# One decoder block on one core: the attention output is multiplied by its norm before the output projection, and the memory values are formed 512 columns wide

## The chip, the cores and the metric

The kernel runs on one core of a Trainium2 chip. The metric is device time in microseconds (us) of one execution. The runs shown before the change took 800.42, 800.91 and 801.06 us, so the median is 800.91 us. All engine times below come from one profiled execution of the same kernel.

## What is computed

The block works on 512 tokens of 1024 features, in float32, in this order:

```python
u  = rmsnorm(h, g_mix)
qa, ka, va, qb, kb, vb = split(u @ w_in)            # 16 heads of 64
ya = dilated_attention(qa, ka, va, bias)            # heads 0..7
yb = moba_attention(qb, kb, vb, bias)               # heads 8..15
y  = concat(rmsnorm(ya, g_out_dil), rmsnorm(yb, g_out_moba))
h  = h + y @ w_out
h  = h + cross_attention(rmsnorm(h, g_cross), rmsnorm(mem, g_mem))   # 256 memory tokens, 4 heads
h  = h + w_down(silu(conv3(rmsnorm(h) @ w_gate)) * (rmsnorm(h) @ w_up))
out = rmsnorm(h, g_final)
```

Two norms stand between self-attention and `w_out`: one over the 512 features of heads 0 to 7, one over those of heads 8 to 15. A norm's factor is one number per token and half, so it can be multiplied into `y` before the product, or into the two half products after it.

## The kernel before

Everything is kept with features on the partitions and tokens on the free axis. A float32 product is made of three float32r matmuls: each operand is split into a rounded high part and the rest, and high x high, low x high and high x low are summed in one PSUM bank (`fgroup`, L263 to L268). Such a triple for one slice of 128 input features is called a group here.

**Weights.** `Weights` (L54 to L137) streams chunks of 128 x 1024 numbers through three buffers: a DMA from the queue of SyncE, then ScalarE writes the high part in two halves (L88), then VectorE or GpSimd writes the low part in two halves (L97). `tick(k)` issues these four pieces beside the groups of the chunk in use and stays two chunks ahead.

**Order.** The order of every engine's instructions is the order in which the program issues them. `Later` (L140) holds chains of small operations and issues each stage some steps behind: every group on TensorE ends with `L.step()`, and a stage is issued once its step number is reached. `drain` issues all that is left at once.

**PSUM.** There are eight banks: `acc` 2, `s` 3, `t` 2, `o` 1 (L190). A bank that is asked for again is handed over only when the reads of its former content have ended.

**Self-attention** runs in 18 slots. In slot s the scores of head s (S), the transposes of head s-1 (T) and the value product of head s-2 (O) are issued in the order given by `ORDER`, and between them projections that don't depend on attention are filled in: `fill(x)` issues groups until the count that `PACE` gives for slot x is reached. There are 208 such groups: Q, K and V projections (the first 144), memory keys `km_unit` (32), memory values `vm_unit` (32). `need` issues what is left after the last slot; before the change nothing is left. After a pair of heads, `o_evac` adds up `y`, squares it into a running sum and splits it into `Yh` and `Yl`, without the norm (L762 to L770).

**Memory values** (L574 to L609) are made in four column groups of 256 and two token tiles, one bank each, one after the other: a matmul has 256 columns.

**Output projection** (L819 to L842). Each of eight tiles takes two banks, one for each half of the features. The first is multiplied by the first norm on VectorE (f0) and added to `h` on GpSimd (L832); the second is multiplied by the second norm on VectorE (f1) and added to `h` on VectorE (L840). `resid` then makes the operand of the next product (ScalarE L251, VectorE L261) and the running sum of squares (ScalarE L276, GpSimd L281). The norm factors come from `norm_stages` (L283): a copy and a rest (L290, L294), two matmuls with ones (L301, L302), an inverse square root and a square on ScalarE (L306, L307), and three VectorE operations (L311 to L313). Cross-attention's query projection (`cq_unit`, L848) follows at once; its first tile needs `Xh[7]`, which comes from the last tile of the output projection.

**Later stages.** `w_o` (L984 to L1012) already runs its first three tiles over part of the features, holds them in three banks, and then finishes them.

## Time and profile before

| | |
|---|---|
| median of 3 runs | 800.91 us |
| span of the profiled execution | 799.3 us |
| what lies around the span (median minus span) | 1.6 us |
| groups of memory values left behind the last slot of attention | 0 |
| output projection, first matmul to first matmul of the next product | 260.75 to 305.69 us |

The profile lists no other time for the profiled execution than its span; the three runs stand 1.1 to 1.8 us above it. A matmul's row gives a modelled duration that overlaps the next matmul, so what one costs in a stream is read from the distance between the starts of neighbours, and a wait shows as a larger distance. "Idle before" in square brackets says how long the engine stood still and whom it waited for.

### The profile page before, as it was taken

The page shows a single profiled execution, that of the slowest core. Times are in us where ns is not written, and L with a number is a line of the kernel's source. Part 1 is how long each engine was busy: PE and PEld are TensorE (multiplying, and loading weights), DVE is VectorE, ACT ScalarE, POOL GpSimd, SP SyncE. Part 2 cuts the span into 40 slices and gives each one's busy share as a digit, 9 for nine tenths or more (in the row PEclk, how much of TensorE's full clock was granted, in tenths as well). Part 3 has the DMA queues.
Part 4 walks back from the last instruction along what each step waited for, and adds up shares of the span by engine and source line. Part 5 has one row for each costly group of instructions (what it writes and reads, how often), then busy time and mean ns, then how long its engine had stood idle before and what let it go on. Part 6 is the DMA issues. An engine that isn't in the chain of part 4 may idle for free.

```text
span 799.3 us, 10566 instructions
## 1 busy us (share of the span) xinstructions
PE 776.4 (97%) x3916; PEld 657.2 (82%) x3916; DVE 493.0 (62%) x894; ACT 389.8 (49%) x763; POOL 165.2 (21%) x163
## 2 busy tenths in 40 slices
PE   9999999999999998999999999999999999999995
PEld 7878989878898786888888888888888888888884
DVE  4656677678886987666476756666656664332324
ACT  5866666677767533544255533343334343322322
POOL 1056565663645343000021000000000000000001
PEclk9999999999999998999999999999999999999998
DMA  9544243343434222121033332222232233333303
GB/s 346 192 136 138 91 126 93 120 114 122 146 133 155 83 81 104 55 78 53 26 106 106 107 105 101 84 106 95 90 106 105 80 99 99 99 93 98 100 21 105
DMA packets 27107, 85.85 MB, mean 107 GB/s; under 512 B 3072, under 2 KB 5248, under 8 KB 26672
## 3 DMA queue, kind: packets, MB, share of 16 engines
q1 hardware_dynamic: 25696, 83.90, 31.7%
q10 hardware_dynamic: 1232, 1.12, 0.4%
q8 instruction: 30, 0.49, 0.3%
q14 instruction: 21, 0.17, 0.1%
q0 software_dynamic: 128, 0.17, 0.1%
HBM read 78.84 MB, written 2.14 MB: 101 GB/s over the span
## 4 chain that ended last, share of the span: by engine, by line
PE 77%; DVE 12%; ACT 6%; issue 2%; POOL 2%; DVEq 0%; POOLq 0%; ACTq 0%
PE acc L266 15%; PE acc L267 15%; PE acc L268 15%; PE s L266 5%; PE s L267 5%; PE s L268 5%; DVE lo L97 2%; ACT P L688 2%; DVE P L695 2%; PE o L739 1%; DVE tmp L257 1%; DVE P L683 1%; POOL h L832 1%; PE t L710 1%; ACT hi L88 1%
## 5 line engine op out<-in xcount | busy, mean ns | idle before, releaser
L88 ACT ACTIVATE hi<-stage 128x512 fp32r<-128x512 f32 (+1 forms) x264 | 151.7, 616 | 171.6 <-PE acc L267 130.7
L97 DVE TENSOR_TENSOR lo<-stage,hi 128x512 fp32r<-128x512 f32 (+1 forms) x211 | 156.8, 773 | 57.6 <-ACT hi L88 57.5
L266 PE MATMUL acc<-X,hi 128*128 128x512 f32 (+1 forms) x432 | 167.3, 387 | 3.6 <-ACT X L251 3.4
L268 PE MATMUL acc<-X,lo 128*128 128x512 f32 (+1 forms) x432 | 162.9, 377 | 0.0
L267 PE MATMUL acc<-X,hi 128*128 128x512 f32 (+1 forms) x368 | 137.6, 374 | 1.4 <-DVE X L261 1.2
L266 PEld LDWEIGHTS acc<-X,hi 128*128 128x128 f32 x432 | 82.3, 191 | 16.8 <-ACT X L251 3.8
L268 PEld LDWEIGHTS acc<-X,lo 128*128 128x128 f32 x432 | 82.1, 190 | 15.0
L267 PEld LDWEIGHTS acc<-X,hi 128*128 128x128 f32 x368 | 69.8, 190 | 12.6 <-DVE X L261 2.5
L97 POOL TENSOR_TENSOR lo<-stage,hi 128x512 fp32r<-128x512 f32 x53 | 71.6, 1368 | 27.3 <-ACT hi L88 25.7
L266 PE MATMUL acc<-G,hi 128*128 128x512 f32 (+1 forms) x198 | 72.9, 368 | 0.0
L268 PE MATMUL acc<-G,lo 128*128 128x512 f32 (+1 forms) x198 | 72.3, 365 | 0.0
L267 PE MATMUL acc<-G,hi 128*128 128x512 f32 (+1 forms) x198 | 72.3, 365 | 0.0
L266 PE MATMUL s<-X,hi 128*128 128x512 f32 x176 | 68.5, 389 | 0.0
L267 PE MATMUL s<-X,hi 128*128 128x512 f32 x176 | 68.5, 389 | 0.0
L268 PE MATMUL s<-X,lo 128*128 128x512 f32 x176 | 68.5, 389 | 0.0
L688 ACT ACTIVATE P<-P,st 128x512 f32<-128x512 f32 (+1 forms) x64 | 35.6, 557 | 39.9 <-DVE st L683 39.7
L1042 DVE SCALAR_TENSOR_TENSOR c<-a,vec,c 128x512 f32<-128x512 f32 x44 | 33.1, 752 | 24.6 <-ACT c L1037 23.8
L1032 POOL MEMSET a<- 128x2 f32 x22 | 2.1, 100 | 210.3 <-DVE c L1042 210.3
L281 POOL TENSOR_TENSOR ss<-ss,tmp 128x512 f32<-128x512 f32 x14 | 18.2, 1298 | 123.9 <-ACT tmp L276 123.9
L266 PEld LDWEIGHTS acc<-G,hi 128*128 128x128 f32 x198 | 37.3, 188 | 6.2
L267 PEld LDWEIGHTS acc<-G,hi 128*128 128x128 f32 x198 | 37.3, 188 | 6.1
L268 PEld LDWEIGHTS acc<-G,lo 128*128 128x128 f32 x198 | 37.3, 188 | 5.9
(242 smaller groups left out, 1516.4 us busy)
## 6 DMA issues: line engine op xcount, KB each, us to landing
stage<-in_w_gu_dram SPq DMA_DIRECT2D x44, 512.0 KB, 3.3
stage<-in_w_in_dram SPq DMA_DIRECT2D x23, 512.0 KB, 3.4
stage<-in_w_dn_dram SPq DMA_DIRECT2D x16, 512.0 KB, 3.5
strip<-scr SPq DMA_DIRECT2D x16, 256.0 KB, 3.6
stage<-in_w_km_dram SPq DMA_DIRECT2D x8, 512.0 KB, 3.9
stage<-in_w_vm_dram SPq DMA_DIRECT2D x8, 512.0 KB, 3.3
stage<-in_w_out_dram SPq DMA_DIRECT2D x8, 512.0 KB, 3.2
stage<-in_w_q_dram SPq DMA_DIRECT2D x8, 512.0 KB, 3.2
```

Of the source, the lines that this page charges most:

```text
L88: self.nc.scalar.activation(self.hi[i][:, a:b], self.stage[i][:, a:b], AF.Copy)
L97: self.lo_eng[part].tensor_sub(self.lo[i][:, a:b], self.stage[i][:, a:b], bf(self.hi[i][:, a:b]))
L257: nc.vector.tensor_mul(dst, a, b)
L266: nc.tensor.matmul(ps, wh[:, w0:w0 + P], xh, start=first, stop=False)
L267: nc.tensor.matmul(ps, wh[:, w0:w0 + P], xl, start=False, stop=False)
L268: nc.tensor.matmul(ps, wl[:, w0:w0 + P], xh, start=False, stop=last)
L281: eng.tensor_add(ssq, ssq, q)
L683: nc.vector.tensor_tensor_reduce(v, src, sb[:, :n][:, ::-1], -0.125, 3e38, OP.add, OP.min, accum_out=st[:, i:i + 1])
L688: nc.scalar.activation(v, v, AF.Exp, scale=-1.0, bias=st[:, i:i + 1], accum_out=st[:, 4 + i:5 + i])
L695: engs[NME[i]].tensor_scalar(v, v, st[:, 8 + i:9 + i], None, op0=OP.mult)
L710: nc.tensor.transpose(ps[:, c * P:(c + 1) * P], pt[:, PO[i] + kb * P:PO[i] + (kb + 1) * P], ident)
L1042: nc.vector.scalar_tensor_tensor(v["c"], v["a"][:, 6 + o:6 + o + S], col(C_CW + o * FT + f), v["c"], op0=OP.mult, op1=OP.add)
```

## The change

`o_evac` no longer splits `y`. It keeps all eight `y` tiles. At the end of slot 10 the first norm is formed, and the four tiles of the first half are multiplied by it and split, 24, 36, 48 and 60 steps later. Behind the last slot the second norm is formed and the four other tiles follow 16 to 19 steps later, all issued by a `drain` ahead of the projection. The output projection uses one bank per tile over all eight slices and one addition; its first three tiles run over slices 0 to 3, are held in three banks, and are finished afterwards. The running sum of squares there is added on VectorE. Memory values use two banks at a time with 512 columns per matmul, and `PACE` ends at 200 in place of 209. The reserve for GpSimd's DMA descriptors is set to 4096.

```diff
-PACE = (..., (11.8, 136), (18, 209))
+PACE = (..., (11.8, 136), (18, 200))
...
-            w = [W.take(), W.take()]
-            for t in range(2):
-                ps = bank("acc")[:, :256]
-                for k in range(KT):
...
+            pst = [bank("acc"), bank("acc")]
+            for k in range(KT):
+                if k % 2 == 0:
+                    wh, wl = W.take()
+                ws = slice((k % 2) * 512, (k % 2) * 512 + 512)
+                for t in range(2):
...
+                    W.tick((0, 1, 3, 4)[k % 2 * 2 + t])
+                    L.step()
+                    yield
...
+        def y_split(p, R, **at):
+            L.chain(lambda: mul(ys[p], ys[p], R),
+                    lambda: copy(Yh[p], ys[p], col(C_OUT + p)),
+                    lambda: scaled_lo(Yl[p], ys[p], col(C_OUT + p), Yh[p]), **at)
...
-                    ys[p] = ap_.tile([P, S], F32, tag="y", bufs=2, name=f"y{p}")
+                    ys[p] = ap_.tile([P, S], F32, tag="y", bufs=8, name=f"y{p}")
...
-                copy(Yh[p], ys[p], col(C_OUT + p))
...
-                scaled_lo(Yl[p], ys[p], col(C_OUT + p), Yh[p])
...
-            if s == 16:
-                ra_tok = L.chain(*norm_stages(SSQ[0], SSQ[0], S, 512), gap=3)
-        need("vm3")
+            if s == 10:
+                L.need(tok["y", 3])
+                L.chain(*norm_stages(SSQ[0], SSQ[0], S, 512), gap=3)
+                for p in range(4):
+                    y_split(p, SSQ[0], d=24 + 12 * p, gap=3)
+        L.need(tok["y", 7])
+        L.chain(*norm_stages(SSQ[1], SSQ[1], S, 512), d=1, gap=3)
+        for p in range(4, 8):
+            y_split(p, SSQ[1], d=12 + p)
         W.lo_eng = (nc.vector, nc.vector)
-        L.need(tok["y", 7])
-        L.need(ra_tok)
-        RA, RB = SSQ[0], SSQ[1]
-        rb_tok = L.chain(*norm_stages(RB, RB, S, 512), d=RBD, gap=2)
+        need("vm1")
+        L.drain()
...
-                add(nc.gpsimd, ssq, v["s"])
+                add(nc.vector, ssq, v["s"])
...
-            pa, pb = bank("acc"), bank("s")
...
+        part = []
+        for m in range(3):
+            w = W.take()
+            ps = bank("acc" if m < 2 else "s")
+            part.append((ps, w))
+            for k in range(4):
+                W.tick((0, 1, 3, 4)[k])
+                wout_mm(ps, w, k)
+            W.hold = True
+        W.hold = False
+        for m in range(3):
+            for k in range(4, KT):
+                wout_mm(*part[m], k)
+            wout_evac(m, part[m][0])
+            if m < 2:
+                W.split()
+        for m in range(3, KT):
...
+            last = wout_evac(m, ps)
...
-        "w_vm": _rows(kv[:, D:], 4, 256),
+        "w_vm": _rows(kv[:, D:], 2, 512),
...
+                     dynamic_dma_scratch_size=4096)
```

`wout_mm` is one `fgroup` and a step. `wout_evac` is one addition of the bank to `h[m]` on VectorE, followed by `resid`.

## Rows read from the trace of the kernel before

**Rows 1.** The page, parts 1 and 3: engines, GpSimd's DMA queue

```profile
PE 776.4 (97%) x3916; PEld 657.2 (82%) x3916; DVE 493.0 (62%) x894; ACT 389.8 (49%) x763; POOL 165.2 (21%) x163
...
q0 software_dynamic: 128, 0.17, 0.1%
```

**Rows 2.** Windows by stage: length, busy us (instructions) per engine, PE clock, DMA

```profile
173.40:184.00 10.60, 10.60 (x58) 9.05 (x57) 7.46 (x19) 7.13 (x17) 5.52 (x5) 1.00 0.51 148
184.00:201.20 17.20, 15.04 (x84) 12.75 (x82) 14.31 (x29) 13.60 (x32) 6.72 (x6) 0.90 0.38 123
201.20:213.00 11.80, 11.76 (x93) 11.50 (x94) 10.75 (x29) 8.17 (x20) 6.18 (x6) 1.00 0.66 218
213.00:226.20 13.20, 12.63 (x100) 12.05 (x98) 10.67 (x26) 10.19 (x25) 7.46 (x6) 1.00 0.28 93
...
260.75:305.70 44.95, 44.31 (x197) 36.35 (x196) 39.70 (x48) 20.02 (x36) 18.05 (x14) 1.00 0.24 83
...
310.45:319.60 9.15, 5.80 (x13) 4.10 (x13) 6.27 (x9) 3.09 (x6) 2.54 (x2) 0.63 0.33 117
396.00:440.00 44.00, 44.00 (x195) 36.11 (x194) 30.86 (x39) 22.89 (x38) 9.17 (x9) 1.00 0.28 96
```

**Rows 3.** Timeline, end of the output projection: start, duration, engine, line, operation

```profile
310.23 0.39 PE L268 MATMUL acc<-X,lo 128*128 128x512 f32 x1
...
311.17 1.26 POOL L832 TENSOR_TENSOR h<-h,tmp 128x512 f32<-128x512 f32 x1 [1.23 <-DVE tmp L257]
312.46 0.69 DVE L840 TENSOR_TENSOR h<-h,tmp 128x512 f32<-128x512 f32 x1 [0.78 <-POOL h L832]
...
313.96 0.80 PE L266 MATMUL acc<-X,hi 128*128 128x512 f32 x1 [3.35 <-ACT X L251]
...
319.61 0.42 PE L267 MATMUL acc<-hla,hi 128*128 128x512 f32 x1
```

**Rows 4.** Timeline of TensorE, memory values: neighbours 256 columns wide

```profile
246.40 0.28 PE L589 MATMUL acc<-hi,X 128*128 128x256 f32 x1
...
247.00 0.28 PE L588 MATMUL acc<-hi,X 128*128 128x256 f32 x1
```

**Rows 5.** Timeline, norm and split operations

```profile
184.05 0.75 DVE L261 SCALAR_TENSOR_TENSOR Y<-y,vec,Y 128x512 fp32r<-128x512 f32 x1
...
263.18 1.78 DVE L261 SCALAR_TENSOR_TENSOR Y<-y,vec,Y 128x512 fp32r<-128x512 f32 x1
...
268.52 0.69 ACT L306 ACTIVATE tmp<-t,small 128x512 f32<-128x512 f32 x1 [1.18 <-PE t L302]
...
320.81 0.69 DVE L311 SCALAR_TENSOR_TENSOR tmp<-t,tmp 128x512 f32<-128x512 f32 x1 [2.98 <-ACT tmp L307]
...
322.60 0.69 DVE L97 TENSOR_TENSOR lo<-stage,hi 128x512 fp32r<-128x512 f32 x1
323.21 0.68 DVE L257 TENSOR_TENSOR tmp<-acc,ss 128x512 f32<-128x512 f32 x1
...
434.60 1.28 ACT L306 ACT_TABLE_LOAD   x1 [0.88 <-PE t L302]
435.90 0.69 ACT L306 ACTIVATE tmp<-t,small 128x512 f32<-128x512 f32 x1
```

**Rows 6.** Timeline of TensorE: waits in attention and before the output projection

```profile
191.19 0.39 PE L267 MATMUL acc<-X,hi 128*128 128x256 f32 x1 [0.80 <-DVE X L261]
201.24 0.50 PE L739 MATMUL o<-pt0h,V 128*128 128x512 f32 x1 [0.84 <-DVE y L760]
242.48 0.39 PE L588 MATMUL acc<-hi,X 128*128 128x256 f32 x1 [1.50 <-DVE vml L261]
267.93 0.50 PE L302 MATMUL t<-tmp,ones 128*128 128x512 f32 x1 [0.64 <-DVE tmp L254]
```

**Rows 7.** Timeline of ScalarE: splits and evictions

```profile
244.51 0.60 ACT L249 ACTIVATE pt0h<-t 128x512 fp32r<-128x512 f32 x1 [1.87 <-PE t L710]
245.09 1.15 ACT L88 ACTIVATE hi<-stage 128x512 fp32r<-128x512 f32 x2
```

More of the change, by code (lines that the diff above doesn't have):

```diff
@@ L32 @@
 ORDER = "OSOTOSTOST"
-PACE = ((0, 8), (1, 17), (1.8, 24), (5.0, 64), (5.85, 72), (9.1, 112), (11.8, 136), (18, 209))
+PACE = ((0, 8), (1, 17), (1.8, 24), (5.0, 64), (5.85, 72), (9.1, 112), (11.8, 136), (18, 200))
 RM = 13
@@ L42 @@
 LOM = "vg"
-RBD = 5
 GS = GQ = GO = (1, 1)
@@ L625, in block_kernel @@
         FILL += [(f"km{m}", km_unit(m)) for m in range(8)]
-        FILL += [(f"vm{c}", vm_unit(c)) for c in range(4)]
+        FILL += [(f"vm{c}", vm_unit(c)) for c in range(2)]
         fill_gen = fillers()
@@ L814, in r1, with wout_mm, wout_evac @@
                 scaled_lo(lo, h[m], col(c + m), hi)
-                add(nc.gpsimd, ssq, v["s"])
+                add(nc.vector, ssq, v["s"])
             return r0, r1
-        for m in range(KT):
-            w = W.take()
-            pa, pb = bank("acc"), bank("s")
-            v = {}
+        def wout_mm(ps, w, k):
+            fgroup(ps, w, k, Yh[k], Yl[k], k == 0, k == KT - 1)
+            L.step()
+        def wout_evac(m, ps):
+            return L.chain(lambda: nc.vector.tensor_add(h[m], h[m], ps),
+                           *resid(m, ss1, Xh[m], HL[m], C_CROSS))
+        part = []
+        for m in range(3):
+            w = W.take()
+            ps = bank("acc" if m < 2 else "s")
[13 more added lines that the diff above has]
+            w = W.take()
+            ps = bank("acc")
             for k in range(KT):
                 W.tick(k)
-                fgroup(pa if k < 4 else pb, w, k, Yh[k], Yl[k], k % 4 == 0, k % 4 == 3)
-                L.step()
-                if k == 3:
-                    def f0(pa=pa, v=v):
-                        v["a"] = tmp()
-                        mul(v["a"], pa, RA)
-                    L.chain(f0, lambda m=m, v=v: nc.gpsimd.tensor_add(h[m], h[m], v["a"]))
-            def f1(pb=pb, v=v):
-                L.need(rb_tok)
-                v["b"] = tmp()
-                mul(v["b"], pb, RB)
-            def f2(m=m, v=v):
-                nc.vector.tensor_add(h[m], h[m], v["b"])
-            last = L.chain(f1, f2, *resid(m, ss1, Xh[m], HL[m], C_CROSS), d=6 if m == 0 else 1)
+                wout_mm(ps, w, k)
+            last = wout_evac(m, ps)
         R1 = ss1
@@ L1226 @@
     from concourse.bass_utils import run_bass_kernel_spmd as _run
-    nc = _bacc.Bacc("TRN2", target_bir_lowering=False, num_devices=1)
+    nc = _bacc.Bacc("TRN2", target_bir_lowering=False, num_devices=1,
+                     dynamic_dma_scratch_size=4096)
     arrays, args = {}, []
```

25 lines of the change are left out of this document (8 added, 17 removed).

## The prediction

> **What bounds the kernel now.** I read the page first. TensorE is busy for 776.4 of 799.3 us [rows 1]. So the number of matmul columns sets most of the time, and a change can win only where columns get cheaper, where TensorE waits, or where it runs at the lower clock. Next come the windows by stage, which say where it waits: from 310.45 to 319.60 TensorE is busy for 5.80 of 9.15 us at a mean clock of 0.63 (the lower level, 1.2 GHz, for most of it), and from 184 to 201.2 for 15.04 of 17.20 us at 0.90, while from 396 to 440 (end of `w_o`, start of the MLP) it never stops [rows 2]. Last I read the timeline in the two bad stretches and laid the starts of neighbouring matmuls side by side: what a distance has above its normal value is lost time, and the row's bracket names whom TensorE waited for.
>
> **What columns cost.** Five matmuls of 256 columns lie between 246.40 and 247.00: 0.120 us each [rows 4]. One of 512 takes 0.226: 195 of them fill 44.00 us without a wait [rows 2], and a group of three takes 0.68. Memory values are 192 matmuls of 256 columns, 23.0 us. They become 96 of 512, 21.7 us. Gain 1.3 us. It could be nothing, if the stationary operand (now memory, with a wider moving one) had another price, or 2 us with the slower first matmul after each switch; I take 1.3, since the rows of 256 columns are of this very loop. The Trainium skill (TensorE: Matmul & The Clock Gate, Back-to-back issue gap) gives an isolated gap of columns over 2.4 GHz plus 2.5 ns, which would leave a gain of only some 0.25 us here (an estimate from that page); the rows have both widths slower than that, and they decide.
>
> **End of the output projection.** The last matmul starts at 310.23. The last tile still needs a product with each norm, the addition on GpSimd (311.17), the addition on VectorE (312.46), and the copy on ScalarE; the next product's last slice starts at 313.96, after 3.35 us idle by the row. Counted from start to start it is 3.5 us late. Then 12 matmuls reach to 319.61: 5.65 us for what takes 2.7 at full clock [rows 3]. Together 6.4 us. Behind this is VectorE: 39.70 us busy of 44.95 in the stage, with GpSimd beside it for 18.05 [rows 2]. Afterwards a tile has one addition, one rest, one running sum and two weight rests on VectorE, 0.61 to 0.67 us apart [rows 5]: 3.2 us of the 5.45 us in which TensorE makes a tile. After the last matmul: eviction 0.2 us later, 0.6 addition, two weight halves of 1.15 us on ScalarE that lie ahead in its queue [rows 7], 0.63 copy, so the operand is there after some 2 us, and TensorE needs it after seven groups, 4.8 us. The stage from 396 to 440 has this form and no wait [rows 2]. The running sum goes to VectorE (seven times 0.61 us), covered by the 2.2 us per tile that it then has free. I take 0.2 us off, since the first bank of the next projection is handed back by a chain that the stall no longer feeds ahead. Gain 6.2 us; 0 if VectorE is late in another way.
>
> **Start of the output projection: what is late next.** Before, TensorE went from attention to the projection with one wait of 0.8 us at the norm's second matmul (0.64 idle, and a first matmul of 0.50 in place of 0.39) [rows 6]; that goes, because the matmul now comes later in the stream. What comes instead is worked out from the queues. `PACE` reaches 198.97 at slot 17.9, so 199 of 208 groups are issued and 9 remain. Seven of them run, then the norm's two matmuls (call their end P), then two more groups: TensorE asks for the projection's first bank at P + 1.36. This bank holds memory values, and their eviction is issued by `drain`, on ScalarE behind the norm's root. From P: 0.35 until ScalarE has the sum (267.93 [rows 6] to 268.52 [rows 5], less a matmul), 1.30 for the table load that precedes the root (434.60 to 435.90; Exp was the last function used), 0.69 root [rows 5], 0.60 each for the square and the copy of the values [rows 7], 0.75 rest [rows 5] and 0.06 to TensorE: the bank is free at P + 4.35. Wait 3.0 us. Behind it, VectorE still has the second rest (0.67), the norm's three operations (1.79, from 320.81 to 322.60), then products and rests of the four tiles: until the last product 4.0 us [rows 5]. Then ScalarE copies that tile (0.7), and only then comes the high part of the projection's third weight chunk (0.62), since `drain` put everything ahead of it: P + 12.05. TensorE has done the first two tiles' halves (8 groups, 5.4 us) at P + 9.8 and waits 2.3 us, then 0.3 more for the low part. Queued behind this wait are all later matmuls. Cost 5.6 us together; 3.0 if the third chunk were split already, 7 if the clock falls after a wait as it did after 3.35 us [rows 3]. Nothing is late after that: the tiles 4 to 7 of `y` are split by then.
>
> The Trainium skill (ScalarE: Activation LUTs, What ACT_TABLE_LOAD costs) puts a switch to another set of functions at about 2.66 us with its drain, and asks to keep functions of one set together, which the norm at slot 10 does not. The rows here have 1.30 from load to root. By the page the wait at the first bank would be 1.4 us longer and the sum would come out at 801.5 (an estimate).
>
> **One new wait inside memory values.** Both `acc` banks change hands at once, at slot 17.2. The eviction of the first is issued one step after the matmul that needs its bank, behind half a weight chunk on ScalarE: 0.62 until that buffer is free (a matmul on, and its 0.39 [rows 3]), 0.57 for the half, 0.60 copy [rows 7], 0.75 rest [rows 5], 0.1 on the way, against cover of one group and one O step, 1.03. Cost 1.6 us; 0.5 to 2.5 by what ScalarE and VectorE hold just then. Where memory keys pass their banks on, 0.2.
>
> **Attention.** Four parts. (a) Slots 3 to 10 lose a copy and a rest per pair (0.75 us of VectorE [rows 5]); waits of the kind at 201.24 [rows 6], of which there are three, shrink. Gain 0.5, between 0 and 1.5, the sum of the three. (b) The wait at 242.48 for a bank (1.50) [rows 6] goes, as memory values change banks only once; what delays the softmax there, the rest of `y`, moves away, so that the transposes behind it wait less. Gain 1.9, between 0.5 and 2.3. (c) In slot 11 ScalarE gets the norm with two table loads, 4.4 us, into 10.6 us of which it works 7.1 [rows 2]; a copy of 0.7 leaves. Cost near 0.5, between 0 and 2. (d) In slots 12 to 14 VectorE gets four products and four rests, 4 x 1.36 = 5.4 us, and loses two rests, 1.5 us. Two of them fall into the stretch in which TensorE already waits for VectorE, at 191.19, and at 201.24 [rows 6]. `PACE` takes 3.2 us of filling out of these slots, with 1.6 us of VectorE work. VectorE had 35.7 us in 42.2 there [rows 2]; it will have 38.0 in 39.0. Some must show as waits: I take 1.7 us, between 0, if the gaps take it, and 6. With (c), 2.2 us.
>
> **At nothing.** The order of DMAs from SyncE stays, with as many chunks of the same size; chunks wait behind the same splits. The smaller descriptor reserve concerns a queue of 128 packets and 0.17 MB [rows 1]; these transfers belong to the first stage, and if their cover were gone it would be a microsecond once. The matmuls of the projection are as many as before. The two products per tile with the norms (16 x 0.61 us) go from VectorE, which hid them behind TensorE.
>
> **The sum.** Gains: 1.3 + 6.2 + 0.8 + 1.9 + 0.5 = 10.7. Costs: 5.6 + 1.6 + 0.2 + 2.2 = 9.6, and 0.3 for a shorter fall of the clock behind the 3 us wait, much of which the next wait takes up: 9.9. Net 0.8 us faster, a span of 798.5 from 799.3. The runs stand 1.6 us above the span, so against the median 800.91 I forecast 800.1 us: no change that can be told. A measurement of this kernel can tell 0.2%, 1.6 us: below 799.3 is faster, above 802.5 slower. The stall at the end of the projection is paid back at its start.
>
> **Rivals.**
>
> *VectorE's gaps take the early splits* (faster). For it: from 184 to 226 VectorE stands idle for 6.5 us [rows 2], and the filling that is taken out relieves it. Then the 2.2 us go, and relief in slots 3 to 10 takes up to 1 us more: 800.1 - 3.2 = 796.9. Against it: the idle time lies in short waits for ScalarE, and a rest beside GpSimd takes 1.78 us, not 0.75 [rows 5].
>
> *VectorE becomes the bound of slots 12 to 14* (slower). It decides once VectorE must work more than 0.85 of the time, its share from 184 to 226 [rows 2]. At that share 38.0 us need 44.7 us in place of 39.0: 5.7, where I counted 1.7, and the clock falls once more as it did from 184 to 201 (0.10 of 17.2 us, 1.7). 800.1 + 4.0 + 1.7, less the part of slot 11 that hides in it (0.5): 805.3; with half of the excess, 802.7.
>
> *The end of the projection doesn't get free.* If the operand were still late, through weight halves ahead of it, 6.2 come back: 806.3. Against it the stage from 396 to 440.
>
> **How the numbers follow.** The forecast gets 0.37: of it 0.27 within 0.2%, 0.07 faster and 0.03 slower by uneven small terms. The faster rival gets 0.35, the slower 0.25, the third 0.03. Faster 0.42, same 0.27, slower 0.31. The likeliest case alone spans 798.5 to 802.5. The range reaches into the cases of both signs: at the lower end the faster rival with a third chunk split in time (796.9 - 2.6 = 794.3, little of it left out), at the upper end the slower rival: 795.0 to 805.5.
>
> **What would show it.** No gap and full clock where query projection starts; two gaps at the start of the output projection, near 3.0 us (for VectorE's rest of memory values) and 2.6 us (for the third chunk's high part); one gap of 1.6 us within memory values; a distance of 0.226 us between all their matmuls; a table load in slot 11 and one right after the norm's matmuls; more waits for VectorE from slot 12 to 14. The prediction is wrong if the two gaps are not there, or if attention as a whole moves by more than 3 us.

## The result and the profile after

The changed kernel takes 811.60 us (810.74 to 813.74), beside 800.98 for the kernel before on the same chip: ratio 1.0126, 95% interval 1.0109 to 1.0143. It is 10.6 us slower, where 800.1 us, no change, was forecast. Its profiled span is 808.9 us against 799.3.

The page's first part, after. In the profile after, most lines of the program stand one number lower than before (L267 there is L268 here [rows 3]).

```profile
PE 779.2 (96%) x3820; PEld 654.0 (81%) x3820; DVE 481.1 (59%) x899; ACT 392.7 (49%) x761; POOL 130.8 (16%) x138
```

There are 96 matmuls fewer and GpSimd works 34 us less [rows 1], but TensorE stands more. The windows by stage, after: length, then busy us (instructions) of PE, PEld, DVE, ACT, POOL, the clock, DMA. The first line is slot 11, the next three are slots 12 to 14, the fifth slot 15, the sixth slot 17 to the first matmul of the output projection, the seventh that projection, the last what follows it.

```profile
172.20:185.20 13.00, 11.70 (x59) 9.11 (x57) 9.02 (x20) 10.90 (x22) 5.90 (x5) 1.00 0.44 125
185.20:205.10 19.90, 14.49 (x72) 11.75 (x72) 16.89 (x35) 14.09 (x31) 7.15 (x6) 0.90 0.36 113
205.10:217.30 12.20, 12.20 (x86) 11.86 (x87) 10.37 (x27) 8.95 (x22) 4.83 (x4) 0.88 0.48 162
217.30:230.80 13.50, 12.17 (x94) 11.40 (x92) 12.58 (x29) 8.55 (x22) 7.94 (x6) 1.00 0.28 84
230.80:247.00 16.20, 12.64 (x74) 11.31 (x75) 12.22 (x31) 10.85 (x27) 5.66 (x5) 0.89 0.27 94
256.30:275.06 18.76, 14.80 (x66) 11.36 (x64) 9.48 (x14) 11.79 (x20) 4.32 (x3) 1.00 0.42 141
275.06:321.50 46.44, 45.84 (x192) 37.13 (x193) 30.77 (x48) 20.07 (x34) 0.00 (x0) 0.96 0.25 86
321.50:330.00 8.50, 8.50 (x39) 7.02 (x39) 4.54 (x7) 4.99 (x9) 0.00 (x0) 1.00 0.33 125
```

The last line answers to 310.45 to 319.60 before [rows 2]: what was 5.80 busy of 9.15 us at clock 0.63 is without a gap at full clock. Slots 12 to 14 last 45.6 us where they took 42.2 [rows 2], with some 25 matmuls fewer in them (TensorE's instructions 249 for 274).

The large waits of TensorE, after:

```profile
176.73 0.50 PE L301 MATMUL t<-tmp,ones 128*128 128x512 f32 x1 [0.76 <-DVE tmp L253]
...
185.20 0.50 PE L742 MATMUL o<-pt0h,V 128*128 128x512 f32 x1 [0.54 <-DVE y L763]
...
205.06 0.80 PE L742 MATMUL o<-pt0h,V 128*128 128x512 f32 x1 [2.94 <-DVE y L763]
...
242.70 0.80 PE L588 MATMUL acc<-hi,X 128*128 128x512 f32 x1 [3.55 <-DVE tmp L256]
...
260.22 0.50 PE L588 MATMUL acc<-hi,X 128*128 128x512 f32 x1 [1.56 <-DVE vml L260]
...
275.06 0.50 PE L265 MATMUL acc<-Y,hi 128*128 128x512 f32 x1 [2.32 <-DVE vml L260]
...
282.91 0.50 PE L265 MATMUL s<-Y,hi 128*128 128x512 f32 x1 [0.47 <-ACT hi L87]
...
321.31 0.39 PE L267 MATMUL acc<-Y,lo 128*128 128x512 f32 x1
321.54 0.39 PE L265 MATMUL acc<-X,hi 128*128 128x512 f32 x1
```

The last two rows are where the 3.35 us wait stood [rows 3]: now 0.23 us from one product to the next. The first two rows are of slot 11, which took 10.6 us before [rows 2] and takes 13.0 now, with the early norm in it: its second matmul waits 0.76 us, and at the end of the slot the bank of attention's output is late. The next two rows are the surprise: the wait for `y` was 0.84 before [rows 6], and the 3.55 us where the memory's keys pass their banks to the wide values was not there.

**Lost time by stage.** For each matmul I took the distance to the next start, less what that width takes undisturbed (0.227 us for 512 columns, 0.175 for 384, 0.120 for 256, 0.100 for a transpose), and summed it over the stage, from all rows of TensorE's timeline. It holds waits and the lower clock together. The columns e4, e12, e17 and e9 are experiments that are described below.

| lost us | before | after | e4 | e12 | e17 | e9 |
|---|---|---|---|---|---|---|
| slots 11, 12 | 5.3 | 11.4 | 6.6 | 5.4 | 10.4 | 5.3 |
| slots 13, 14 | 1.1 | 3.4 | 3.4 | 1.1 | 3.3 | 1.3 |
| slots 15, 16 | 2.5 | 5.7 | 5.5 | 6.9 | 0.7 | 1.8 |
| slot 17 to first matmul of the projection | 0.0 | 4.8 | 1.9 | 4.7 | 5.7 | 0.1 |
| within the projection | 1.0 | 3.0 | 0.0 | 2.6 | 7.0 | 2.2 |
| first 20 us of the next product | 7.1 | 0.9 | 6.9 | 6.1 | 0.9 | 1.4 |
| everything else | 13.6 | 12.1 | 15.1 | 14.4 | 12.2 | 14.5 |
| sum | 30.5 | 41.2 | 39.4 | 41.1 | 40.1 | 26.5 |

**Why `y` came late in slot 12.** VectorE and GpSimd, after, ahead of the matmul at 205.06:

```profile
201.98 1.42 POOL L497 TENSOR_TENSOR K<-tmp,K 64x512 fp32r<-64x512 f32 x1 [9.85 <-ACT K L248]
202.17 1.77 DVE L256 TENSOR_TENSOR y<-y,ssy 128x512 f32<-128x512 f32 x1
...
203.87 0.54 DVE L253 TENSOR_TENSOR pt1l<-t,pt1h 128x384 fp32r<-128x384 f32 x1
...
204.33 0.67 DVE L763 TENSOR_TENSOR y<-o,tmp 64x512 f32<-64x512 f32 x1
```

The second row is one of the four early products of `y` with its norm. It was forecast at 0.61 us and took 1.77, and GpSimd had begun a subtraction 0.19 us earlier; the addition that clears the one bank for attention's output is two places behind it. The product explains only part of the wait, though. The experiments below have 2.19 us at this place without any early split (e4 and e2, filling 200), and 1.06 and 1.85 us with the early splits and full filling (e17, e5). So the shorter filling by itself makes most of such a wait.

**Why the keys' bank came late in slot 15.** VectorE, after, ahead of the matmul at 242.70:

```profile
240.38 0.54 DVE L679 CUSTOM_DVE_ANT_0 P<-s,strip 128x384 f32<-128x384 f32 x1
...
241.70 0.17 DVE L689 RECIPROCAL st<-st 128x1 f32<-128x1 f32 x1 [0.77 <-ACT P L684]
241.90 0.42 DVE L691 TENSOR_SCALAR P<-P,st 128x384 f32<-128x384 f32 x1
...
242.23 0.42 DVE L256 TENSOR_TENSOR tmp<-acc,rm 128x256 f32<-128x256 f32 x1
```

The eviction at 242.23, which frees the bank, takes 0.42 us, but stands in order behind a softmax tile, and so behind VectorE's stand for ScalarE's exponential.

### The profile page after: what moved, and what is told of

It reads as the page before. It is cut to its first block, busy times and chain, and to the rows that moved or that the text cites. A ratio compares the mean times of both kernels' runs of the same rounds, so it can differ in the third digit from the quotient of the medians.

```text
span 808.9 us, 10313 instructions
## 1 busy us (share of the span) xinstructions
PE 779.2 (96%) x3820; PEld 654.0 (81%) x3820; DVE 481.1 (59%) x899; ACT 392.7 (49%) x761; POOL 130.8 (16%) x138
## 4 chain that ended last, share of the span: by engine, by line
PE 64%; DVE 2%; ACT 1%; DVEq 0%; issue 0%; ACTq 0%
PE acc L265 15%; PE acc L266 14%; PE acc L267 14%; PE s L267 5%; PE s L266 5%; PE s L265 5%; PE s L899 0%; PE s L898 0%; PE s L897 0%; PE t L926 0%; PE acc L588 0%; PE acc L589 0%; PE acc L590 0%; DVE vml L260 0%; ACT hi L87 0%; DVE y L256 0%
## 5 line engine op out<-in xcount | busy, mean ns | idle before, releaser
L96 DVE TENSOR_TENSOR lo<-stage,hi 128x512 fp32r<-128x512 f32 x214 | 141.2, 694 | 66.6 <-ACT hi L87 66.5
L267 PE MATMUL acc<-X,lo 128*128 128x512 f32 (+1 forms) x432 | 162.3, 376 | 0.0
L267 PEld LDWEIGHTS acc<-X,lo 128*128 128x128 f32 x432 | 81.8, 189 | 14.8
L265 PEld LDWEIGHTS acc<-X,hi 128*128 128x128 f32 x432 | 82.1, 190 | 13.6 <-DVE tmp L256 1.0
L267 PE MATMUL acc<-G,lo 128*128 128x512 f32 (+1 forms) x198 | 72.4, 366 | 0.0
L96 POOL TENSOR_TENSOR lo<-stage,hi 128x512 fp32r<-128x512 f32 x50 | 67.3, 1363 | 22.7 <-ACT hi L87 15.5
L267 PE MATMUL s<-X,lo 128*128 128x512 f32 x176 | 68.5, 389 | 0.0
L265 PE MATMUL acc<-Y,hi 128*128 128x512 f32 x112 | 44.8, 400 | 2.3 <-DVE vml L260 2.3
L267 PE MATMUL acc<-Y,lo 128*128 128x512 f32 x112 | 44.3, 396 | 0.0
L266 PE MATMUL acc<-Y,hi 128*128 128x512 f32 x112 | 44.2, 395 | 0.0
L265 PEld LDWEIGHTS acc<-G,hi 128*128 128x128 f32 x198 | 37.3, 188 | 6.2
```

Of the source, the lines that this page charges most:

```text
L96: self.lo_eng[part].tensor_sub(self.lo[i][:, a:b], self.stage[i][:, a:b], bf(self.hi[i][:, a:b]))
L265: nc.tensor.matmul(ps, wh[:, w0:w0 + P], xh, start=first, stop=False)
L266: nc.tensor.matmul(ps, wh[:, w0:w0 + P], xl, start=False, stop=False)
L267: nc.tensor.matmul(ps, wl[:, w0:w0 + P], xh, start=False, stop=last)
```

## The experiments

Ratios are to the kernel before, measured beside it on the same chip. "Before" and "after" say which kernel the edit is made in.

### One part of the change alone, or undone

**e1_banks** (after): the two wide banks of memory values from two pools.

```diff
-            pst = [bank("acc"), bank("acc")]
+            pst = [bank("acc"), bank("s")]
```

> The changed kernel, but the second bank of a memory-value unit comes from the three banks of tag s, so that no bank of memory values is asked for while its former content is still to be read. Theory (bank hand-over): the wait of 3.7 us in slot 15 for the eviction of the last memory keys, with the slow clock behind it (1.2), and the 1.7 us between the two memory-value units vanish; the wait of 2.5 us at the first bank of the output projection goes too, but comes back at the third weight chunk, whose splits stand behind the same chain. So about 7 us faster than the changed kernel: 804.5 us. Rival (VectorE is late in any case, the bank only shows it): the next transposes or value products wait instead, and 2 us at most are won: 809.5 or more.

809.35 us, 1.0093 [1.0078, 1.0108], 2.3 us better than after: close to the rival and far from the theory's 7. The loss of slot 17 falls from 4.8 to 0.4 and slot 15's from 5.6 to 3.1, where TensorE now waits 2.47 us for `y` (244.59), and the projection's third weight chunk is late:

```profile
280.16 0.71 PE L265 MATMUL s<-Y,hi 128*128 128x512 f32 x1 [4.73 <-ACT hi L87]
```

The banks are real waits, and each covered the next one.

**e2_late** (after): norm and splits of the first half of `y` in slot 15 and later, not from slot 11.

```diff
-            if s == 10:
-                L.need(tok["y", 3])
+            if s == 15:
...
-                    y_split(p, SSQ[0], d=24 + 12 * p, gap=3)
+                    y_split(p, SSQ[0], d=15 + 3 * p, gap=2)
```

> The changed kernel, but the first norm and the four splits of the first half are issued at the end of slot 15 (splits 15, 18, 21, 24 steps on) in place of slot 10. Theory (early splits overload VectorE in slots 11 to 14): the loss there, 14.8 us in the changed kernel, falls back to about the 6.4 us of the kernel before, and slots 16 and 17 take the work for 1 to 2 us: 805 us. Rival (the shorter filling by PACE starves those slots): the loss stays, within 2 us: 810 or more.

812.30 us, 1.0131 [1.0116, 1.0146]. The time is the rival's, the place the theory's: slots 11 and 12 lose 5.8 us again in place of 11.4, so it was the early norm and splits that cost them 5.6 us, some 2 of it in slot 11, which is 10.6 us long again. The work then stands in front of other things: slots 15 and 16 lose 9.7, slot 17 5.3, the projection 4.6.

**e3_vm256** (after): memory values again 256 columns wide, with the loop, the weight layout and `need("vm3")` of before.

```diff
-            pst = [bank("acc"), bank("acc")]
...
+            w = [W.take(), W.take()]
+            for t in range(2):
+                ps = bank("acc")[:, :256]
```

> The changed kernel with memory values in four groups of 256 columns as before (8 groups still left behind attention). Theory (bank hand-over): slot 15 loses its 5.5 us, the 1.7 us between units go, and 1.3 us of columns come back; the wait ahead of the output projection stays: 806 us. Rival (columns: the wide form is a gain and the waits move elsewhere): 811 to 813 us.

813.17 us, 1.0143 [1.0125, 1.0160]: the rival, just beyond its range. Slot 17 loses 1.7 in place of 4.8, the projection 7.1 in place of 3.0. Slots 15 and 16 lose as much as in the kernel after (5.9 for 5.7) although no two banks change hands at once there: TensorE waits 3.44 us for `y` instead (246.04).

**e4_pace200** (before): only the shorter filling.

```diff
-PACE = (..., (11.8, 136), (18, 209))
+PACE = (..., (11.8, 136), (18, 200))
```

> The kernel before with the last point of PACE at 200 in place of 209, nothing else: 9 groups run behind the last slot. Theory (early splits are the cause in slots 11 to 14): hardly any loss from this alone, 800.5 to 802.5 us. Rival (less filling starves attention): most of the 8.4 us of slots 11 to 14 show up here: 806 us or more.

808.84 us, 1.0086 [1.0071, 1.0101]: the rival, 6.9 us slower by this line alone. TensorE waits long for `y` at the ends of slots 12 and 15, with no early split and no wide value in the kernel:

```profile
202.19 0.79 PE L739 MATMUL o<-pt0h,V 128*128 128x512 f32 x1 [2.19 <-DVE y L760]
...
242.61 0.50 PE L739 MATMUL o<-pt0h,V 128*128 128x512 f32 x1 [3.44 <-DVE y L760]
```

Slots 12 to 14 with 24 matmuls fewer are no shorter; the windows of e4 and, for later, of e13 and e18:

```profile
185.20:227.90 42.70, 37.29 (x250) 33.69 (x249) 35.87 (x81) 29.67 (x71) 17.64 (x16) 0.96 0.41 125
```

```profile
184.30:227.00 42.70, 36.84 (x250) 33.71 (x248) 34.88 (x72) 29.46 (x70) 27.19 (x23) 0.96 0.40 125
```

```profile
184.20:226.80 42.60, 36.88 (x251) 33.29 (x250) 35.78 (x79) 29.51 (x71) 17.71 (x16) 0.96 0.40 126
```

All three last 42.6 or 42.7 us, where the kernel before took 42.2 with 274 matmuls. VectorE's groups in these slots point to a reason. Of the kernel before, from 184 to 226.2 (busy us, mean ns | idle time ahead of the group, and what ended it):

```profile
L261 DVE SCALAR_TENSOR_TENSOR X<-stage,vec,X 128x256 fp32r<-128x256 f32 x8 | 5.3, 688 | 0.5 <-ACT X L251 0.5
L683 DVE CUSTOM_DVE_ANT_0 P<-s,strip 128x512 f32<-128x512 f32 (+3 forms) x11 | 5.2, 484 | 0.0
...
L257 DVE TENSOR_TENSOR tmp<-acc,rm 128x256 f32<-128x256 f32 x6 | 2.5, 413 | 0.0
...
L693 DVE RECIPROCAL st<-st 128x1 f32<-128x1 f32 (+1 forms) x9 | 1.5, 163 | 4.8 <-ACT P L688 4.8
```

The groups that take something from TensorE (scores, banks) have 0.0 idle ahead of them: by the profile VectorE never waits for TensorE here. It is busy 35.7 us and idle 6.4 (the sum of this column over all groups), 4.8 of it in front of the reciprocal, for ScalarE's exponential. So in the kernel before the filling in these slots was free: something else already made them as long as they are. That this is VectorE's queue with its stand for ScalarE is my reading; the experiments on slots 12 to 17 test it. What is taken out comes back behind attention as time of its own, 9 units of it.

**e5_pace209** (after): filling as before.

```diff
-PACE = (..., (18, 200))
+PACE = (..., (18, 209))
```

> The changed kernel with PACE ending at 209 again: all filling inside attention, nothing left behind it. Theory (in slots 12 to 17 the length of a slot is set by VectorE's queue, so filling that is taken out is lost): those slots get about 6 us back, but the second norm's chain now has no groups of memory values beside it, so some 6 us more are waited for at the start of the output projection: 809 to 813 us. Rival (the loss in attention was the early splits' after all, and the filling is only moved): slots 13 to 16 keep their loss of 9 us and the front waits 6 us more: 817 us.

814.26 us, 1.0154 [1.0137, 1.0171]: worse, and between theory and rival. Slots 11 to 14 lose 14.2 (after 14.8), so the shorter filling did not cause that loss; it covered the start of the projection, where now 12.6 us are lost (slot 17 and projection) in place of 7.7. But here filling is not free: slots 12 to 14 last 47.9 us in place of 45.6, so the 24 or 25 matmuls that come back into them, 2.9 us at 0.120 each, cost 2.2.

**e12_vm512_same_banks** (before): only the wide memory values, in two banks of one pool, filling as before.

> The kernel before with memory values 512 columns wide in two banks of the one pool that the projections use, as in the changed kernel, with filling as before. It prices the passing on of the banks alone, against 799.75 us with banks from two pools. Theory: the first wide unit has to wait for both banks of the last two tiles of the memory's keys, and the second unit and the projection for the evictions of the ones ahead: 1 to 3 us where the keys pass theirs on, some 1.6 us between the units, and 1 to 3 us at the start of the projection: 802.5 to 806 us. Rival: with full filling VectorE reaches these evictions in time, and the banks cost what the prediction took, 0.2 + 1.6 us: 800.5 to 802 us.

809.10 us, 1.0101 [1.0087, 1.0114], 8.1 us slower: beyond the theory's range. TensorE's waits in it:

```profile
231.79 0.50 PE L588 MATMUL acc<-hi,X 128*128 128x512 f32 x1 [1.83 <-DVE tmp L257]
...
250.52 0.50 PE L588 MATMUL acc<-hi,X 128*128 128x512 f32 x1 [1.90 <-DVE vml L261]
...
268.88 0.80 PE L266 MATMUL acc<-Y,hi 128*128 128x512 f32 x1 [4.45 <-DVE vml L261]
```

Keys to values, values to values, values to projection: each time both banks change hands, and the first is asked for before VectorE has come to its eviction.

**e7_b_vm512** (before): the same, but the banks from two pools.

```diff
+            pst = [bank("acc"), bank("s")]
```

> The kernel before with memory values 512 columns wide, the second bank from tag s, PACE as before. Theory (columns cost what the rows show, and the banks are the only price of the wide form): 1.3 us of columns and the wait of 1.7 us for a bank in slot 16 are won: 798.0 to 799.5 us. Rival (attention has no room for it, other waits come): 801 or more.

799.75 us, 0.9979 [0.9970, 0.9988]: 1.7 us faster, which is short of the theory's range. The wait for a bank at 242.48 [rows 6] is gone, but the transposes there now wait 0.48 and 0.57 us, so that slots 15 and 16 still lose 2.0 us in place of 2.5. That leaves 1.2 for the columns, about the forecast's 1.3. By the ratios the choice of the second bank is worth 1.2% there, 9.8 us; in the changed kernel it was worth 2.3.

**e17_y_part** (after): filling 209 and banks from two pools, which leaves `y` times its norm, its early splits and one bank per tile.

> The changed kernel with filling up to 209 as before and the banks of the wide memory values from two pools: what is left of the change is y times its norm ahead of the output projection, the early splits and one bank per tile, over a kernel of 799.75 us. Theory (the parts share covers, so that their costs don't add): slots 11 and 12 lose 6 us to the early splits' work on VectorE, the start of the projection 5 to 6, its end gains 6.2: 803.5 to 806.5 us, and slots 13 to 17 lose less than 6 us. Rival (the early splits by themselves already use up VectorE's room in slots 12 to 17, and filling and banks add nothing to it): 809 us or more, with slots 13 to 17 losing over 8 us.

809.77 us, 1.0112 [1.0095, 1.0129]. The time is the rival's, the place is not: slots 13 to 16 lose 4.0, as e7's 3.2. Slots 11 and 12 lose 10.4 (e7: 5.5), and slots 12 to 14 are as long as in e5:

```profile
184.70:232.50 47.80, 41.99 (x273) 38.03 (x273) 40.67 (x92) 33.63 (x78) 20.61 (x17) 0.93 0.39 123
```

The start of the projection is dear:

```profile
266.88 0.50 PE L300 MATMUL t<-tmp,ones 128*128 128x512 f32 x1 [2.69 <-ACT tmp L248]
269.50 0.79 PE L301 MATMUL t<-tmp,ones 128*128 128x512 f32 x1 [2.12 <-DVE tmp L253]
...
280.40 0.50 PE L265 MATMUL s<-Y,hi 128*128 128x512 f32 x1 [2.57 <-ACT hi L87]
```

With no filling left, nothing covers the second norm's two matmuls, and slot 17 and the projection together lose 12.7 us, for 5.8 gained at its end.

### What holds slots 12 to 17

**e10_pace200_gs2** (before, filling 200) and **e11_gs2** (before): the scaling of a softmax tile two steps behind its exponential.

```diff
-GS = GQ = GO = (1, 1)
+GS, GQ, GO = (1, 2), (1, 1), (1, 1)
```

> The kernel before with two edits: filling up to 200 units only by slot 18 (808.84 us by itself), and the reciprocal and the scaling of a softmax tile two steps behind its exponential instead of one, so that VectorE meets the finished exponential and doesn't stand for it in order. Theory (with less filling, slots 12 to 17 last as long as VectorE's queue in order, which stands some 7.5 us for ScalarE's exponentials there): the waits of VectorE for P fall below 3 us in slots 12 to 17, the loss of these slots (17 us with filling 200) falls by 3 to 6 us, 803 to 806 us. Rival (it is not VectorE's stand but the chain from scores to transposed scores, its stages one after the other, that sets the slots): a later scaling makes this chain longer, 808.5 us or more.

> The control: the kernel before with only the scaling of the softmax tiles two steps behind the exponential. Theory: with full filling TensorE loses under 9 us in slots 12 to 17, most of it in slot 12 and by the clock, so there is little to gain: 799.5 to 801.5 us. Rival (the chain of stages sets the slots): 803 us or more.

e10: 812.62 us, 1.0146 [1.0132, 1.0160]; e11: 803.96, 1.0037 [1.0025, 1.0050]. Both times are the rival's, in which the chain from scores to transposed scores sets the slots: the stand itself is not what could be saved. In e11's slots 12 to 14 VectorE's idle time for the exponential falls from 4.8 to 1.4 us, and the slots last 42.5 us, as long as before, its busy time being 38.2 in place of 35.7. In e10 the wait for `y` in slot 12 is 3.01 us (2.19 in e4), and transposes wait 1.67 for the later scaling.

**e13_pace200_lo_pool** (before, filling 200), **e14_lo_pool** (before), **e15_after_lo_pool** (after) and **e16_best_lo_pool** (e9): the low halves of the weight chunks, from the memory's keys to the end of attention, all on GpSimd.

```diff
-LOM = "vg"
+LOM = "gg"
```

> The kernel before with filling 200, and the low halves of the weight chunks from the memory's keys to the end of attention both split on GpSimd, where one half was VectorE's (12 splits of 0.80 us in slots 12 to 16). Theory (VectorE's work in order ahead of the eviction of the output bank makes the wait): the two waits of TensorE for the addition of y (2.35 and 3.59 us with filling 200 alone) fall below 1 us each, and 808.84 us becomes 803 to 806. Rival (the chain of stages as such, or GpSimd, which then scales the softmax tiles later): 808 us or more.

> The control: the kernel before, filling as it was, with the low halves of these weight chunks both split on GpSimd. Theory: with full filling the waits for VectorE are under 1 us each in these slots outside slot 12, so it gains little, 799 to 801.5 us. Rival (GpSimd in order, its splits ahead of the scaling that the transposes wait for): 803 us or more.

> The changed kernel with the low halves of these weight chunks both split on GpSimd. Theory: the wait of 2.94 us for y in slot 12 and that of 3.55 us where the memory's keys pass their banks on shrink by half or more, since VectorE has some 8 us less to do there: 811.6 us becomes 806 to 808.5. Rival (chain of stages, or GpSimd in order): 811 us or more.

> The fastest version (wide memory values with banks from two pools, and the projection's additions on VectorE; 795.26 us) with the low halves of these weight chunks both split on GpSimd. Theory: it follows the control, within 1 us of 795.3. Rival: GpSimd, now free of the projection's additions, still delays the scaling in attention: 797 us or more.

e13: 805.70 us, 1.0055 [1.0042, 1.0068]; e14: 799.55, 0.9973 [0.9963, 0.9983]; e15: 809.12, 1.0095 [1.0081, 1.0109]; e16: 796.08, 0.9936 [0.9923, 0.9948]. e13's time is as the theory said, its waits only by half: 2.35 us of loss in front of `o` at the end of slot 12 stays, the other goes from 3.59 to 2.10. e14 gains 2.2 us by the ratio, within the theory's range. e15 gains 2.5, less than the 3.1 to 5.6 of the theory, and its two waits shrink by a quarter (2.18 and 2.66 us), not by half. e16 gains nothing over e9. Slots 12 to 14 did not get shorter (the windows above): seven splits of 0.86 us left VectorE, but it is busy 34.9 us in place of 35.9. The same groups in e4 and in e13:

```profile
L261 DVE SCALAR_TENSOR_TENSOR X<-stage,vec,X 128x256 fp32r<-128x256 f32 x8 | 5.3, 687 | 0.5 <-ACT X L251 0.5
L254 DVE TENSOR_TENSOR X<-tmp,X 128x256 fp32r<-128x256 f32 x5 | 3.2, 641 | 0.0
L257 DVE TENSOR_TENSOR tmp<-acc,rm 128x256 f32<-128x256 f32 x5 | 2.1, 417 | 0.0
```

```profile
L261 DVE SCALAR_TENSOR_TENSOR X<-stage,vec,X 128x256 fp32r<-128x256 f32 x8 | 7.2, 924 | 0.5 <-ACT X L251 0.5
L254 DVE TENSOR_TENSOR X<-tmp,X 128x256 fp32r<-128x256 f32 x5 | 6.6, 1321 | 1.1 <-ACT X L249 1.0
L257 DVE TENSOR_TENSOR tmp<-acc,rm 128x256 f32<-128x256 f32 x5 | 2.1, 418 | 0.0
```

The first two groups have both operands in SBUF and got 5.3 us longer; the third reads a bank of PSUM and didn't change. What GpSimd took over it took back from VectorE's other work, so e13 relieved VectorE by 1 us there, and does not test the theory in slot 12.

**e18_pace200_o2** (before, filling 200): two banks for attention's output, two for scores.

```diff
-        banks = {"acc": 2, "s": 3, "t": 2, "o": 1}
+        banks = {"acc": 2, "s": 2, "t": 2, "o": 2}
...
-        vps = [bank("s"), bank("s"), bank("s"), bank("o")]
+        vps = [bank("s"), bank("s"), bank("o"), bank("o")]
```

> The kernel before with filling 200, and two banks for the output of attention in place of one, taken from the scores, which have two in place of three (the first statistics' fourth tile goes to the second output bank). Theory (with less filling between two heads TensorE reaches the next head's output before VectorE has cleared the one bank): the waits of 2.35 and 3.59 us in front of an output go, and slots 12 to 16 lose 9 to 12 us in place of 15.3. Rival (the bank is only where TensorE waits first, and with it free it waits as long for the transposed scores or for a bank of the scores): slots 12 to 16 lose 14 us or more, with the waits in front of transposes or scores.

808.74 us, 1.0092 [1.0077, 1.0106], as e4; slots 12 to 16 lose 16.0 us (e4: 15.3). The rival: the two waits in front of an output are gone, and TensorE waits as long for the next link.

```profile
217.79 0.33 PE L710 MATMUL t<-ident,P 128*128 128x128 f32 x1 [1.93 <-POOL P L695]
...
244.74 0.33 PE L710 MATMUL t<-ident,P 128*128 128x128 f32 x1 [3.34 <-POOL P L695]
```

### The start and the end of the projection, and the fastest version

**e6_front** (after, banks from two pools): the second and third tile in banks of the scores, and `drain` with the norm's splits behind the first halves of the three tiles.

```diff
-            ps = bank("acc" if m < 2 else "s")
+            ps = bank("acc" if m < 1 else "s")
```

> The changed kernel with the bank edit of e1, the second and third projection tiles in banks of tag s, and the drain moved behind the first three half tiles, so that the third chunk's splits are issued ahead of the products and rests of y. Theory (at the start of the projection TensorE waits only for orders of issue: a bank behind the norm's root, a chunk behind the splits): against e1 the loss at the start of the projection, 6.7 us, falls under 1.5: 803.5 to 804.5 us. Rival (the chain from the second norm to the splits of y is too long whatever the order): slices 4 to 7 wait instead and under 2.5 us are won: 807 or more.

806.77 us, 1.0066 [1.0051, 1.0081], 2.6 better than e1: near the rival. The third chunk is in time; TensorE waits for a split of `y` instead (1.29 us at 280.05), and the projection loses 4.2 us for 6.7.

**e8_b_dveadd** (before): the two additions per tile on VectorE.

```diff
-                    L.chain(f0, lambda m=m, v=v: nc.gpsimd.tensor_add(h[m], h[m], v["a"]))
+                    L.chain(f0, lambda m=m, v=v: nc.vector.tensor_add(h[m], h[m], v["a"]))
...
-                add(nc.gpsimd, ssq, v["s"])
+                add(nc.vector, ssq, v["s"])
```

> The kernel before with the two additions per tile in its output projection on VectorE in place of GpSimd. Theory (the wait at the end of the projection comes from VectorE held up beside GpSimd and from the long way over two engines): the 6.4 us at the end shrink to 3 or less: 797 to 799 us. Rival (VectorE has no room for two more operations per tile, 4.9 of 5.45 us): the wait stays or grows: 801 to 804 us.

796.54 us, 0.9940 [0.9925, 0.9955]: the theory, and slightly better. VectorE has more operations in the projection, but at 0.68 to 0.75 us each, and the next product's first 20 us lose 1.4 us in place of 7.1. So most of the end's 6.2 us was GpSimd's additions, and can be had without moving `y`.

**e9_best**: e7 and e8 together.

> The kernel before with the two edits that helped by themselves: memory values 512 columns wide with their two banks from different pools (-1.3 us alone), and both additions of the output projection's tiles on VectorE instead of GpSimd (-4.5 us alone). Theory: they lie in different stages (slots 13 to 17, and the end of the projection), so they add: 794.5 to 796.0 us, no wait over 1 us at the start of the cross-attention's queries. Rival: the wider values leave their last eviction to VectorE where the projection starts, and the additions on VectorE meet it: 797 us or more, with the difference in waits in the first three tiles of the projection.

795.26 us, 0.9929 [0.9916, 0.9943]: faster than both kernels, and the two gains add, as the theory said. From 173.9 to the projection, which here is 85.6 us (87.35 before, 102.9 after), the mean clock is 1.00:

```profile
173.90:259.50 85.60, 81.06 (x493) 70.82 (x492) 65.36 (x147) 62.62 (x139) 43.90 (x36) 1.00 0.44 142
```

## Why the prediction was wrong

Its terms, and what the lost time by stage says they were:

| term | forecast | measured | from |
|---|---|---|---|
| end of the projection free | -6.2 | -6.2 | 7.1 to 0.9 |
| columns | -1.3 | -1.3 | 96 x 0.227 us for 192 x 0.120 |
| norm's second matmul, (a) slots 3 to 10 | -1.3 | -2.1 | 0.96 to 0.24; start to slot 10: 11.1 to 9.8 |
| start of the projection | +5.6 | +5.4 | 2.48 ahead of it, 2.95 within |
| between the units of values | +1.6 | +1.7 | 260.22 |
| (b) bank and `y` in slots 15 to 17 | -1.9 | -1.6 | rest of these slots |
| keys pass their banks on | +0.2 | +5.2 | 242.70 and the lower clock behind it |
| (c) norm in slot 11 | +0.5 | +1.9 | 0.2 to 2.1 |
| (d) slots 12 to 14 | +1.7 | +6.5 | rest of 6.4 to 14.8 |

The 0.3 us that the forecast had for the clock has no row: what the lower clock took stands with the waits ahead of it. The prediction named a move of attention by more than 3 us as a sign that it is wrong; the loss of slots 11 to 16 went from 8.9 to 20.5 us.

**Right.** The end of the projection gets free and is paid back at its start, in the places named. The first bank waits 2.5 us (3.0 forecast); the third chunk shows 0.5 of its 2.3 us, because TensorE was at the lower clock from 276.4 to 279.8 and so arrived 1.6 us later; the sum is off by 0.2. The table loads came in slot 11 (178.64 and 181.30) and right after the norm's matmuls (271.00), each 1.28 us. The smaller descriptor reserve, put at nothing, was not changed by itself in any run; up to slot 10 the kernel after loses less than before (9.8 for 11.1), so no cost of it shows.

**The step that failed: "(d)".** It let slots 12 to 14 go from 42.2 to 39.0 us, since "`PACE` takes 3.2 us of filling out of these slots", and added 1.7 us of new waits for the early splits, 40.7 in all. They became 45.6. The larger error is in the early splits. With full filling they take these slots from 42.2 to 47.8 us (e17): 5.6 where 1.7 was counted. They do not fall into gaps; VectorE's idle time in these slots is a stand in order, for ScalarE (the view under e4). e2, which moves the early norm and the splits out, gives slots 11 and 12 back 5.6 us of loss. The smaller error is in the filling. Taking it out brings 2.2 us back beside the early splits (47.8 to 45.6), and nothing without them: e4 has 42.7 us with 24 matmuls fewer. The forecast's slower rival, VectorE as the bound of slots 12 to 14, with 44.7 us and a fall of the clock, came nearest; I gave it 0.25. It too was short: VectorE came to 39.8 us of work (16.89 + 10.37 + 12.58 in the windows) where I counted 38.0; the four products with the norm alone took 3.8 us where 2.4 were counted.

**Two terms that were mis-sized.** "(c)", "Cost near 0.5", measured 1.9: ScalarE's room was counted, but not that the norm's second matmul waits for its operand here too (0.76 us, the kind of wait that the forecast had booked as a gain at the other norm) and that `y` comes late (0.54). And "Where memory keys pass their banks on, 0.2" is 3.7 us of wait and 1.5 at the lower clock. I priced the eviction's duration and not its place in VectorE's queue, behind a softmax tile. e12 shows this without the rest of the change: 1.98 us there, and against e7 9.8 us in all for this choice of banks. But the bank alone does not explain what slots 15 and 16 lose in the kernel after. They lose 5.7 us there, 4.8 with banks from two pools (e1), 6.4 with full filling (e5), and 0.7 only with both (e17). The shorter filling alone (e4) and the shared pool alone (e12) each bring this loss to the kernel before as well: 5.5 and 6.9 for 2.5.

By the profiled spans the forecast missed by 10.4 us (9.6 slower for 0.8 faster; by the medians 11.5). Slots 11 to 14 make 6.2 of it, the keys' banks 5.0, and the other terms together take 0.8 back.

**What the parts cost one by one** is not what they cost together: shorter filling +6.9 (e4), wide values in one pool +8.1 (e12), the part with `y` about +10.6 over e7 (1.0112 to 0.9979, of 801 us), sum 25.6; together 10.1 by the ratio. The values left behind attention by the shorter filling cover the norm's matmuls that e17 has bare, and a bank waited for here gives a chunk waited for later its time (e1, e3).

**Still open.** What sets the length of slots 12 to 14 is not shown. For VectorE's queue with its round trips to ScalarE stand its idle time, the one length of 42.2 to 42.7 us that five kernels have there (before, e4, e11, e13, e18), and e2, whose rests of `y` stand later: 41.3 us. Against it stands that the rival of e10 and e11, the chain of stages from scores to transposed scores, had the right time in both, and that in e18 the wait only moved to the next link of that chain. Nor is the kernel after settled: there, too, VectorE never waits for TensorE, and yet the full filling of e17 makes slots 12 to 14 2.2 us longer, while VectorE's work grows by 0.8 (39.84 to 40.67). No run relieved VectorE by much and it alone: e11 and e13 took a stand or work away and got longer operations in return. Nor was the clock changed by itself: the stretches at the lower level that are new in the kernel after (from 205, 242 and 276 us on) stand behind waits, and are counted with them.

## What to carry to other kernels

Before work is moved into or out of a pipelined stage, ask the idle time of each engine whom it waits for. If the in-order engine beside TensorE never waits for TensorE, taking TensorE's work out of that stage may gain nothing, as in e4; it is a hint and no proof, since in the changed kernel the same view goes with filling that did cost time (e5). Then take the filling out alone and look at the length of the stage. Price a bank by the place of its eviction in the evicting engine's queue, not by the eviction's duration, and take the next tile's bank from another pool where both would change hands at once. Test each part of a bundled change alone, and two that may cover each other in all four combinations: here two edits, wide values with banks from two pools and the projection's additions on VectorE, held all the gain, and two others each made most of the same loss.

## What the runs showed of the hardware

**In these runs operations of VectorE with both operands in SBUF stretch beside GpSimd; those that read PSUM don't.** From e4 to e13 the means go from 641 to 1321 ns and from 687 to 924, with GpSimd busy for 27.2 us in place of 17.6 of 42.7, and stay at 417 and 418 for a bank. Single cases end with GpSimd's operation: it began at 201.98 and took 1.42, and VectorE's product, begun at 202.17, took 1.77, to 0.54 us after it. In the kernel before, one of 1.62 us began at 262.79, and VectorE's rest, begun at 263.18, took 1.78 [rows 5], to 0.55 us after it. The Trainium skill (SBUF — State Buffer, Who interferes with whom) says that an operation of VectorE with two SBUF inputs and one of GpSimd that reads SBUF exclude each other, the second waiting until the first is done; the rows agree. Seven splits of 0.86 us moved from VectorE to GpSimd took 1.0 us off VectorE's busy time in slots 12 to 14 of e13.

**The lower clock follows some waits and not others.** Three windows of the kernel after, each right behind a wait: of 2.94, of 3.55 and of 1.56 us.

```profile
205.00:208.40 3.40, 3.34 (x12) 3.00 (x13) 2.69 (x10) 2.82 (x8) 1.94 (x3) 0.54 0.77 261
242.60:246.00 3.40, 3.30 (x10) 2.79 (x11) 2.39 (x9) 2.69 (x7) 0.82 (x1) 0.55 0.00 0
260.20:263.60 3.40, 3.38 (x16) 2.79 (x17) 2.25 (x2) 0.53 (x2) 1.29 (x1) 1.00 0.24 83
```

The first two stretches run at 0.54 and 0.55 of full clock, the 1.2 GHz level for most of them, with 0.43 us between matmuls of 512 columns; the third at full clock. The length of the wait alone does not decide: in e1 full clock follows a wait of 2.47 us (1.00 from 244.5 to 248.0), in e4 the lower level one of 2.19 us (0.51 from 202.1 to 205.5). Behind each of the first two waits the lower level cost 1.5 us, and behind the 3.35 us of the kernel before some 3 us (5.65 for 2.7 [rows 3]). The forecast had 0.3 for all of that.
